# Two tiles in front of the split gated activations get more unused columns

## The chip, the cores and the metric

The kernel runs on one core of one Trainium2 chip. The metric is the device time of one execution in microseconds: 899.65 us as the median of three runs (899.22 to 900.09). One execution was also taken by the hardware profiler; it took 898.85 us, and its trace spans 897.0 us from the first to the last instruction, so 1.85 us lie around the span.

## The reference, cut to what matters

A decoder trunk of two layers works on 256 positions of width 2048 in float32. Each layer has the same wiring:

```
hn = rmsnorm(h, norm_g[l])
z  = hn @ w_in                       # one combined input projection
y  = concat(head outputs) * silu(gate)
h  = h + y @ w_out                   # one output projection
```

Layer 0 has dilated attention heads beside gated linear attention (GLA) heads. Layer 1 has S5 state-space channels beside HGRN2 heads, and its S5 output passes through one more product with a 1024x1024 matrix (`s5_w_glu`). The last step is a final rmsnorm. In this document "gated activation" means `y`, the left operand of the output projection.

## The kernel before, in words

Every large product is made of three TensorE products in the type fp32r. A float32 operand is split into a high part, rounded to fp32r, and a low part, the rest; high times high, high times low and low times high are added up in PSUM. The normalised input is held as `xh` and `xl` (split by `split_x`, L205 and L206), the gated activation as `yh` and `yl`, and a weight tile as `wh` (ScalarE, L168) and `wl` (VectorE, L169), both made from `raw`, which a DMA on SyncE's queue fills 1 MB at a time. All four activation tiles have 16 k-tiles of 256 columns, so one k-tile is 1024 bytes of a partition.

Two helpers run these products. `gemm_fm` (matmuls on L181) makes a block of 512 features by 256 positions: the weight slice of 128x128 is stationary (it is loaded into the array) and the activation k-tile of 256 columns moves. A group in it is 4 k-tiles, and one k-tile is 12 matmuls: three products by four weight slices. `gemm_tm` (L200) makes a block of 256 positions by 512 features: a 128x128 slice of the activation is stationary and 512 weight columns move. The last quarter of the last projection is written out by hand with the same operands in 256 columns (`mms`, L756): in its first half the moving operand is a weight tile `wh` or `wl`, in its second half the moving weights lie in the memory of `xh` and `xl`, which are free by then.

The gated activations are used in these places, and nowhere else on TensorE:

- `out_proj` of layer 0, four blocks of `gemm_fm` with 16 k-tiles: 4 x 16 x 12 = 768 matmuls, with `yh` or `yl` as moving operand.
- the S5 product (`I["wg"]`), two blocks of `gemm_fm` with 8 k-tiles: 192 matmuls, `yh` or `yl` moving.
- the output projection of layer 1, three blocks of `gemm_tm`: 3 x 16 x 6 = 288 matmuls, `yh` or `yl` stationary.
- its last quarter (L756): 192 matmuls, `yh` or `yl` stationary.

The order of instructions on each engine is fixed when the program is built. Small float32 matmuls of the mixers (attention, GLA, S5) and of the norms are put between the large ones in many places, so the stream of large matmuls is cut into stretches.

Tiles lie in SBUF one behind the other in the order of their pools, each rounded up to 32 bytes. This gives the start of each tile in a partition; what matters of the layout of the kernel before is:

| tile | starts at byte | modulo 512 | what lies in front |
|---|---|---|---|
| `hT` (inside `xv`) | 17,392 | 496 | `vec` |
| `xh`, `xl` | 33,792 and 50,176 | 0 | `xv` |
| `wh`, `wl` buffers | from 124,736, each 4096 long | 320 | `raw` |
| `pT` (attention, 392 columns) | 191,520 | 32 | `qk` |
| `yh`, `yl` of layer 0 | 193,088 and 209,472 | 64 | `pT` |
| S5 preparation tiles of layer 0 | from 193,088 | 64 | `pT` |
| gates of layer 0 (in `gq` and `gk`) | 155,456 and 159,552 | 320 | `gf` |
| `gz0`, `gz1` (gates of layer 1; `gz1` has 1048 columns) | 181,280 and 185,376 | 32 | `small` tiles |
| S5 tiles of layer 1 (`tb`, `X`, `t0`...) | from 189,568 | 128 | `gz1` |
| `yh`, `yl` of layer 1 | 189,568 and 205,952 | 128 | `gz1` |

The S5 preparation uses the same memory as `yh` of layer 0 before it, and the S5 tiles the same as `yh` of layer 1. A slice that is a stationary operand (128 columns, 512 bytes) starts at the same place modulo 512 as its tile.

Of the kernel before, what the change touches and what calls it, by code (L numbers as in the profile page):

```python
# [12 lines left out]
F32 = mybir.dt.float32  # L13
# [7 lines left out]
S = 256  # L21
# [36 lines left out]
def trunk(ctx: ExitStack, tc: tile.TileContext, I, out):  # L58
# [13 lines left out]
    def urgent():  # L72
        return tc.high_priority(offset=HI)
# [16 lines left out]
    def pm_tile(name="pm"):  # L90
        return pm.tile([128, 512], F32, name=name, tag="pm")
# [21 lines left out]
    def finish_norm(tag):  # L113
        V.tensor_add(sqa[:, 0:2], sqa[:, 0:2], sqa[:, 2:4])
        V.tensor_add(sqa[:, 0], sqa[:, 0], sqa[:, 1])
        ps = pm_tile()
        for t in range(2):
            T.matmul(ps[:, t:t + 1], sqa[:, 0, t * 128:(t + 1) * 128], ones[:, 0:1], start=True, stop=True)
        ms = small.tile([128, 2], F32, name="nms")
        V.tensor_scalar(ms, ps[:, 0:2], 1.0 / D, EPS, op0=OP.mult, op1=OP.add)  # L120
        rc = const.tile([128, 2], F32, name=tag + "c")
        rsqrt(rc, ms, 2, "nr")
        pb = pm_tile()
        for t in range(2):
            dg = small.tile([128, 128], F32, name="dg")
            V.tensor_scalar(dg, ident, rc[:, t:t + 1], None, op0=OP.mult)
            T.matmul(pb[:, t * 128:(t + 1) * 128], ones, dg, start=True, stop=True)
        rb = const.tile([128, S], F32, name=tag + "b")
        A.activation(rb, pb[:, 0:S], AF.Copy)
        return rc, rb  # L130
# [62 lines left out]
    def gemm_tm(src, groups, ah, al, mid=None, order=None):  # L193
        ps = pg.tile([128, 2, 512], F32, name="pg")
        last = groups * 4 - 1
        for i, kt, wh, wl in _iter(src, groups, mid, order):
            for n, (w, a) in enumerate(((wh, ah), (wh, al), (wl, ah))):
                for t in range(2):
                    ts_ = slice(t * 128, (t + 1) * 128)
                    state["mm"] = T.matmul(ps[:, t], a[:, kt, ts_], w, start=(i == 0 and n == 0),  # L200
                                           stop=(i == last and n == 2), skip_group_check=True)
        return ps
# [8 lines left out]
    def gla_tiles():  # L211
        return (mix.tile([128, 4, S], F32, name="gf"), mix.tile([128, 4, S], F32, name="gq"),
                mix.tile([128, 4, S], F32, name="gk"))

    att = ExitStack()
    ap_ = att.enter_context(tc.tile_pool(name="att", bufs=1))
# [23 lines left out]
    f, q, k = gla_tiles()  # L240
# [167 lines left out]
    def attention(h, q, k, v, vc):  # L408
        pr = ap_.tile([128, 2, S], F32, name="pr", bufs=1)
        mx = small.tile([128, 2], F32, name="amx")  # L410
        den = small.tile([128, 2], F32, name="aden")
        ps = pm_tile().rearrange("p (t j) -> p t j", t=2)
        for t in range(2):
            n = 128 * (t + 1)
            T.matmul(ps[:, t, 0:n], q[:, t * 128:(t + 1) * 128], k[:, 0:n], start=True, stop=True)  # L415
        for t in range(2):
            n = 128 * (t + 1)
            V.scalar_tensor_tensor(pr[:, t, 0:n], ps[:, t, 0:n], rsc[:, t:t + 1], bias[:, t, 0:n],
                                   op0=OP.mult, op1=OP.add)
            V.tensor_reduce(mx[:, t:t + 1], pr[:, t, 0:n], axis=mybir.AxisListType.X, op=OP.max)  # L420
        V.tensor_scalar(mx, mx, -1.0, None, op0=OP.mult)
        for t in range(2):
            n = 128 * (t + 1)
            A.activation(pr[:, t, 0:n], pr[:, t, 0:n], AF.Exp, bias=mx[:, t:t + 1], accum_out=den[:, t:t + 1])
        V.reciprocal(den, den)
        for t in range(2):
            n = 128 * (t + 1)
            V.tensor_scalar(pr[:, t, 0:n], pr[:, t, 0:n], den[:, t:t + 1], None, op0=OP.mult)
        pt = pm_tile()
        for n, (t, j) in enumerate(((0, 0), (1, 0), (1, 1))):  # L430
            T.transpose(pt[:, n * 128:(n + 1) * 128], pr[:, t, j * 128:(j + 1) * 128], ident)
        pT = ap_.tile([128, 384 + 8], F32, name="pT", bufs=1)[:, 0:384]
        A.activation(pT, pt[:, 0:384], AF.Copy)
        po = pm_tile()
        T.matmul(po[:, 0:256], v[:, 0, vc:vc + 128], pT[:, 0:256], start=True, stop=False)
        T.matmul(po[:, 128:256], v[:, 1, vc:vc + 128], pT[:, 256:384], start=False, stop=True)
        A.activation(oT[:, h], po[:, 0:256], AF.Copy)
# [14 lines left out]
    def heads(qk, h):  # L452
        for n in range(2):
            attention(h + n, qk[:, n], qk[:, 2 + n], v, (h + n) * 128)
# [34 lines left out]
    def gate_tm(src, rc, zs):  # L489
        ps = gemm_tm(src, 4, xh, xl)  # L490
        z = zs.rearrange("p a s -> p (a s)").rearrange("p (t d) -> p t d", t=2)
        with urgent():
            for t in range(2):
                A.activation(z[:, t], ps[:, t], AF.Silu, scale=rc[:, t:t + 1])
        return z
# [34 lines left out]
    with urgent():  # L530
        rc1, rb1 = finish_norm("r1")
# [3 lines left out]
    w1 = I["w1"]  # L535
    gz = ctx.enter_context(tc.tile_pool(name="gz", bufs=1))
# [124 lines left out]
    for half in range(2):  # L661
        f, q, k = gla_tiles()
# [4 lines left out]
        for n in range(4):  # L667
# [3 lines left out]
        v = mix.tile([128, 2, 512], F32, name="gv")  # L671
        evac_tm(v, 0, gemm_tm(w1[4 + 3 * half], 4, xh, xl), rc1)
        gla(f, q, k, v, 128, 512 * half)
    zs2 = [gate_tm(w1[10 + n], rc1, gz.tile([128, 4 * S + 24 * n], F32, name=f"gz{n}")[:, 0:4 * S]
                   .rearrange("p (a s) -> p a s", a=4)) for n in range(2)]
    while fillq:
        hook()
# [441 lines left out]
def build(arrays):  # L1119
    nc = bacc.Bacc("TRN2", target_bir_lowering=False, num_devices=1)  # L1120
    I = {k: nc.dram_tensor("in_" + k + "_dram", v.shape, mybir.dt.from_np(v.dtype), kind="ExternalInput").ap()
         for k, v in arrays.items()}
    out = nc.dram_tensor("out_0_dram", (2, 128, D), F32, kind="ExternalOutput").ap()
    with tile.TileContext(nc, schedule_with_timeline_sim=True) as tc:
        trunk(tc, I, out)
    if not nc.is_finalized():
        nc.finalize()
    return nc
# [8 lines left out]
```

## Time and profile before

| | |
|---|---|
| median of three runs | 899.65 us |
| the profiled execution | 898.85 us |
| its span | 897.0 us |
| TensorE (PE) busy | 880.9 us, 98% of the span |
| weight loads (PEld), beside the matmuls | 806.7 us, 90% |
| VectorE (DVE) busy | 636.2 us, 71% |
| ScalarE (ACT) busy | 472.5 us, 53% |
| GpSimd (POOL) busy | 54.4 us, 6% |

A matmul's own duration (about 0.28 us for 256 columns) is longer than the time from its start to the start of the next one, since they are pipelined. What one matmul costs the engine is therefore read from starts: a timeline row gives the start of a group of matmuls, and the difference of two starts over the number of matmuls between them is the interval. PEld is the load of the stationary operand, which runs beside the matmul before it. The granted clock is 1.00 in every stage below but the last.

### The profile page before, as it was taken

Reading aid. Unit: us, or ns where it says so; the run is one execution under the profiler, and the core shown is the slowest. Engines: PE = TensorE matmul, PEld = TensorE weight load, DVE = VectorE, ACT = ScalarE, POOL = GpSimd, SP = SyncE. Lnnn points to the kernel's source line nnn. Section 1 sums busy time; section 2 is a strip of 40 time slices with the busy share of each in tenths; the row PEclk is TensorE's granted clock in tenths of the full one; section 3 lists DMA queues with packets and bytes.
Section 4 is the critical chain, followed back from the end, with each engine's and each line's share of the span. In section 5 each row is a group of like instructions: output and inputs, shape, how many; then the busy total and the mean of one; then the engine's idle time right before and its main releaser. Section 6 shows DMA issues by size and latency. Waiting matters only on the chain.

```text
span 897.0 us, 18689 instructions
## 1 busy us (share of the span) xinstructions
PE 880.9 (98%) x7728; PEld 806.7 (90%) x7728; DVE 636.2 (71%) x1197; ACT 472.5 (53%) x715; POOL 54.4 (6%) x106
## 2 busy tenths in 40 slices
PE   8999999999999999999999999999999999999995
PEld 8987799889998899999999998799877899988894
DVE  7987975889869758756575677776987756665562
ACT  7654546665746756544443335455455475544451
POOL 0001100111101001000000001100110000000000
PEclk9999999999999999999999999999999999999998
DMA  9837744777667546544476665754654554554532
GB/s 317 317 100 213 255 164 143 235 254 236 230 210 257 188 168 230 192 176 177 176 277 225 218 245 188 247 191 165 224 165 152 190 189 175 200 180 172 176 132 94
DMA packets 40388, 180.40 MB, mean 201 GB/s; under 512 B 12720, under 2 KB 14256, under 8 KB 22768
## 3 DMA queue, kind: packets, MB, share of 16 engines
q1 hardware_dynamic: 29440, 154.99, 49.0%
q0 software_dynamic: 7984, 22.69, 7.8%
q10 hardware_dynamic: 2880, 1.54, 0.6%
q8 instruction: 60, 0.98, 0.4%
q14 instruction: 24, 0.20, 0.1%
HBM read 166.48 MB, written 12.71 MB: 200 GB/s over the span
## 4 chain that ended last, share of the span: by engine, by line
PE 88%; DVE 4%; DMA 2%; ACT 2%; issue 2%; SPq 0%; POOL 0%; POOLq 0%; DVEq 0%
PE pg L181 51%; PE pg L200 26%; PE pg L756 2%; PE pm L287 1%; PE pm L339 1%; PE pm L621 1%; DMA E<-ed 1%; PE pm L625 1%; DVE wl L169 1%; DMA raw<-in_w_dram 1%; PE pm L583 1%; PE pm L308 1%; PE pm L415 1%; PE pm L1025 1%; ACT wh L168 1%
## 5 line engine op out<-in xcount | busy, mean ns | idle before, releaser
L168 ACT ACTIVATE wh<-raw 128x1024 fp32r<-128x1024 f32 (+2 forms) x276 | 287.7, 1045 | 324.8 <-PE pg L181 192.4
L169 DVE TENSOR_TENSOR wl<-raw,wh 128x1024 fp32r<-128x1024 f32 (+2 forms) x276 | 332.3, 1206 | 171.5 <-ACT wh L168 166.6
L181 PE MATMUL pg<-xh,wh 128*128 128x256 f32 x1024 | 161.8, 279 | 2.3 <-ACT wh L168 2.3
L181 PE MATMUL pg<-xh,wl 128*128 128x256 f32 x1024 | 163.1, 280 | 0.1
L181 PE MATMUL pg<-xl,wh 128*128 128x256 f32 x1024 | 161.1, 278 | 0.0
L181 PEld LDWEIGHTS pg<-xh,wh 128*128 128x128 f32 x1024 | 136.6, 188 | 4.0 <-ACT wh L168 3.4
L181 PEld LDWEIGHTS pg<-xh,wl 128*128 128x128 f32 x1024 | 136.9, 188 | 1.3 <-DVE wl L169 0.5
L181 PEld LDWEIGHTS pg<-xl,wh 128*128 128x128 f32 x1024 | 136.7, 188 | 0.6 <-issue 0.3
L200 PE MATMUL pg<-wl,xh 128*128 128x512 f32 x320 | 101.0, 396 | 0.7 <-DVE wl L169 0.5
L200 PE MATMUL pg<-wh,xl 128*128 128x512 f32 x320 | 100.7, 394 | 0.0
L200 PE MATMUL pg<-wh,xh 128*128 128x512 f32 x320 | 100.3, 394 | 0.0
L200 PEld LDWEIGHTS pg<-wl,xh 128*128 128x128 f32 x320 | 59.1, 188 | 14.2 <-DVE wl L169 1.6
L200 PEld LDWEIGHTS pg<-wh,xl 128*128 128x128 f32 x320 | 59.8, 188 | 12.9
L200 PEld LDWEIGHTS pg<-wh,xh 128*128 128x128 f32 x320 | 59.3, 188 | 12.8
L181 PE MATMUL pg<-yh,wh 128*128 128x256 f32 x320 | 51.8, 283 | 0.0
L181 PE MATMUL pg<-yh,wl 128*128 128x256 f32 x320 | 51.3, 282 | 0.0
L181 PE MATMUL pg<-yl,wh 128*128 128x256 f32 x320 | 51.3, 282 | 0.0
L181 PEld LDWEIGHTS pg<-yh,wh 128*128 128x128 f32 x320 | 44.1, 191 | 0.0
L181 PEld LDWEIGHTS pg<-yl,wh 128*128 128x128 f32 x320 | 44.0, 191 | 0.0
L181 PEld LDWEIGHTS pg<-yh,wl 128*128 128x128 f32 x320 | 44.0, 191 | 0.0
L965 POOL DMA_DIRECT2D tabs<-pc x44 | 23.8, 546 | 164.9 <-DVE x L975 43.3
L200 PE MATMUL pg<-wh,yh 128*128 128x512 f32 x96 | 30.4, 397 | 0.0
(350 smaller groups left out, 1008.4 us busy)
## 6 DMA issues: line engine op xcount, KB each, us to landing
raw<-in_w_dram SPq DMA_DIRECT2D x100, 1024.0 KB, 4.9
raw<-in_wo_dram SPq DMA_DIRECT2D x28, 1024.0 KB, 4.8
tb<-tabs POOLq DMA_DIRECT2D x8, 768.0 KB, 6.5
tabs<-pc POOLq DMA_DIRECT2D x20, 256.0 KB, 5.4
raw<-in_wg_dram SPq DMA_DIRECT2D x4, 1024.0 KB, 4.8
raw<-in_wo1l_dram SPq DMA_DIRECT2D x4, 1024.0 KB, 4.8
raw<-in_w_dram SPq DMA_DIRECT2D x6, 512.0 KB, 7.5
tabs<-pc POOLq DMA_DIRECT2D x24, 128.0 KB, 4.5
```

Of the source, the lines that this page charges most:

```text
L168: state["wh"] = A.activation(w, r, AF.Copy)
L169: V.tensor_sub(l, r, w)
L181: state["mm"] = T.matmul(ps[:, c], w[:, cs], a[:, kt], start=(i == 0 and n == 0 and c % 2 == 0), stop=(i == last and n == 2), skip_group_c ...
L200: state["mm"] = T.matmul(ps[:, t], a[:, kt, ts_], w, start=(i == 0 and n == 0), stop=(i == last and n == 2), skip_group_check=True)
L287: T.matmul(ps[32 * b:32 * b + 32, t, hd], k[:, hd, r], Q[:, hd, r], start=True, stop=True)
L308: T.matmul(ps[j0:j0 + h, hd, j0 + h:j0 + 2 * h], k[:, hd, b:b + h], Qp[:, hd, b + h:b + 2 * h], start=True, stop=True)
L339: T.matmul(ps[:, (hd - h0) * dv:(hd - h0 + 1) * dv], AT[:, hd, t + j], v[:, j, hd * dv:(hd + 1) * dv], start=(j == 0), stop=(j == t))
L415: T.matmul(ps[:, t, 0:n], q[:, t * 128:(t + 1) * 128], k[:, 0:n], start=True, stop=True)
L583: T.matmul(pv[g * 64:g * 64 + 64, w, pr], t["W"][w][us, 4 * h + pr], X[us, g, 4 * h + pr], start=True, stop=True)
L621: T.matmul(py[g * 64:g * 64 + 64, pr], w[:, pr], X[:, g, pr], start=(pr == 0), stop=False, skip_group_check=True)
L756: T.matmul(ps[:, t, 0:256], a_[:, kt, ts_], w_, start=(kt == 0 and n == 0), stop=(kt == KT - 1 and n == 2), skip_group_check=True)
L965: nc.gpsimd.dma_start(tabs[qt, dst, n], t[src].rearrange("p a b -> p (a b)"))
```

## The change

The attention tile `pT` is allocated with 120 unused columns behind its 384 instead of 8, and `gz1` with 120 unused columns behind its 1024 instead of 24 (`gz0` has none either way).

```diff
-        pT = ap_.tile([128, 384 + 8], F32, name="pT", bufs=1)[:, 0:384]
+        pT = ap_.tile([128, 384 + 120], F32, name="pT", bufs=1)[:, 0:384]
...
-    zs2 = [gate_tm(w1[10 + n], rc1, gz.tile([128, 4 * S + 24 * n], F32, name=f"gz{n}")[:, 0:4 * S]
+    zs2 = [gate_tm(w1[10 + n], rc1, gz.tile([128, 4 * S + 120 * n], F32, name=f"gz{n}")[:, 0:4 * S]
```

In layer 0 what lies behind `pT` moves by 112 columns, 448 bytes: `yh` starts at 193,536 = 378 x 512. In layer 1 what lies behind `gz1` moves by 96 columns, 384 bytes: `yh` starts at 189,952 = 371 x 512. The S5 preparation tiles move with the first, the S5 tiles with the second. No instruction is added, taken away or given another size.

## Rows read from the trace of the kernel before

**Rows 1.** The page: busy time of engines, and the chain that ended last by engine.
```profile
PE 880.9 (98%) x7728; PEld 806.7 (90%) x7728; DVE 636.2 (71%) x1197; ACT 472.5 (53%) x715; POOL 54.4 (6%) x106
PE 88%; DVE 4%; DMA 2%; ACT 2%; issue 2%; SPq 0%; POOL 0%; POOLq 0%; DVEq 0%
```

**Rows 2.** By stage (start:end, us): PE, PEld, DVE, ACT, POOL busy (instructions), clock, DMA.
```profile
361.20:453.30 92.10, 92.10 (x770) 92.10 (x769) 55.20 (x62) 44.64 (x52) 0.00 (x0) 1.00 0.51 184
721.30:747.50 26.20, 26.20 (x227) 26.20 (x226) 14.21 (x24) 17.84 (x42) 0.59 (x1) 1.00 0.55 201
793.60:862.60 69.00, 69.00 (x308) 55.68 (x308) 37.84 (x39) 33.18 (x41) 0.00 (x0) 1.00 0.51 183
```

**Rows 3.** Waits in 361.2 to 453.3 us: total us, times, longest.
```profile
ACT wh L168 <- PE pg L181: 42.6, 25, 1.8
```

**Rows 4.** Timeline of PE, layer 0, entering and near the end of the output projection.
```profile
360.27 0.62 PE L181 MATMUL pg<-xh,wl 128*128 128x256 f32 x4
360.73 0.63 PE L181 MATMUL pg<-yh,wh 128*128 128x256 f32 x4
...
362.15 0.64 PE L181 MATMUL pg<-yh,wh 128*128 128x256 f32 x4
...
451.43 0.64 PE L181 MATMUL pg<-yh,wh 128*128 128x256 f32 x4
```

**Rows 5.** The same for the S5 product of layer 1.
```profile
729.12 0.63 PE L181 MATMUL pg<-yl,wh 128*128 128x256 f32 x4
...
746.08 0.63 PE L181 MATMUL pg<-yl,wh 128*128 128x256 f32 x4
```

**Rows 6.** The gate blocks right behind it: first matmuls, and two later ones.
```profile
747.02 1.91 PE L504 MATMUL pm<-cst,gz 128*128 128x128 f32 x16
748.69 0.71 PE L181 MATMUL pg<-xh,wh 128*128 128x256 f32 x4
...
750.15 0.62 PE L181 MATMUL pg<-xh,wh 128*128 128x256 f32 x4
...
790.95 0.62 PE L181 MATMUL pg<-xh,wh 128*128 128x256 f32 x4
```

**Rows 7.** A stretch with xh behind small matmuls of the norm, layer 1.
```profile
464.02 0.36 PE L118 MATMUL pm<-ones,sqa 128*128 128x1 f32 x2
...
465.62 0.63 PE L181 MATMUL pg<-xh,wh 128*128 128x256 f32 x4
...
471.28 0.63 PE L181 MATMUL pg<-xh,wh 128*128 128x256 f32 x4
```

**Rows 8.** L200, moving 512 columns: stationary xh (layer 0), stationary yh (layer 1).
```profile
167.74 0.62 PE L200 MATMUL pg<-wh,xh 128*128 128x512 f32 x2
...
192.46 0.62 PE L200 MATMUL pg<-wh,xh 128*128 128x512 f32 x2
...
795.52 0.63 PE L200 MATMUL pg<-wl,yh 128*128 128x512 f32 x2
...
815.12 0.64 PE L200 MATMUL pg<-wl,yh 128*128 128x512 f32 x2
```

**Rows 9.** L756: first half (two rows), second half (two rows).
```profile
864.31 0.28 PE L756 MATMUL pg<-wl,yh 128*128 128x256 f32 x1
...
871.38 0.28 PE L756 MATMUL pg<-wl,yh 128*128 128x256 f32 x1
...
881.16 0.28 PE L756 MATMUL pg<-xh,yh 128*128 128x256 f32 x1
...
882.94 0.28 PE L756 MATMUL pg<-xh,yh 128*128 128x256 f32 x1
```

**Rows 10.** Groups by line, all 897 us: busy us, mean ns, idle before.
```profile
L583 PE MATMUL pm<-X,tb 64*64 64x64 f32 x256 | 9.3, 221 | 0.0
L504 PE MATMUL pm<-cst,gz 128*128 128x128 f32 x32 | 4.2, 274 | 0.0
L712 PE MATMUL pm<-cst,xv 128*128 128x128 f32 x32 | 4.1, 272 | 0.0
```

## The prediction

> **What bounds the kernel now.** I read the page first. TensorE is busy 98% of the span, and the chain of work that ended last runs through it for 88% [rows 1]. So the time is a sum over matmuls, and what counts is how often a matmul starts. I then looked at the stages that read `yh` and `yl`, by the table of stages: in layer 0's output projection PE is busy for all of 92.1 us, DVE for 55.2 and ACT for 44.6; in the S5 product and in layer 1's output projection PE is busy throughout as well [rows 2]. What feeds PE runs ahead of it: in the first of these stages ScalarE stood for 42.6 us waiting for PE to give a `wh` buffer back [rows 3], so a faster PE finds its weights ready. Last I read the timeline for the interval between starts, and there the operand's place shows.
>
> - Output projection of layer 0 (`yh` moving, at 64 modulo 512): from 362.15 to 451.43 us lie 62 rounds of 12 matmuls, 89.28 us / 744 = 120.0 ns [rows 4].
> - S5 product (`yh` moving, at 128): 16.96 us / 144 = 117.8 ns [rows 5].
> - Gate blocks right behind it, the same code line and the same `wh` buffers, but `xh` moving, at 0: 40.80 us / 360 = 113.3 ns [rows 6].
> - 512 moving columns: 24.72 us / 108 = 228.9 ns with `xh` stationary (at 0), 19.60 us / 84 = 233.3 ns with `yh` stationary (at 128) [rows 8].
>
> The moment of the change is in the trace: the last four `xh` matmuls in front of the output projection start within 0.46 us (115 ns each), and the projection behind them runs at 120 [rows 4]. Weights, PSUM tiles and code line are the same on both sides; the operand is not, and what differs in it is its place (and its values). One row speaks against a rule as simple as "0 is fast": a stretch with `xh` behind the norm's small matmuls runs at 5.66 us / 48 = 117.9 ns [rows 7]. Going through the starts of all 3072 `xh` matmuls of 256 columns I count some 350 at this slow interval, in nine stretches that each begin behind an interruption; nearly all the rest are at 113.3. So an operand at 0 has two intervals, about nine tenths fast, and an operand at 64 was never seen below 120.
>
> **The change, part by part.** No instruction is added or removed; each part is a count times a difference of intervals.
>
> 1. Output projection of layer 0: 768 matmuls move to 0 modulo 512. At the interval of `xh`: 768 x (120.0 - 113.3) ns = 5.1 us. Nothing cuts into this stage, and it is entered from a fast stretch without a gap [rows 4], so I take the fast interval. The other end is the slow one: 768 x (120.0 - 117.9) = 1.6 us. All of it lies on PE's path. What is late next is the split of weights: DVE would work 55.2 us in 87 instead of in 92.1 [rows 2], which is no bound.
> 2. S5 product: 192 matmuls. At 113.3 it is 192 x 4.45 ns = 0.85 us; at the slow interval nothing. It begins behind small matmuls of GLA, and interruptions have led to either (fast behind L504 [rows 6], slow behind L118 [rows 7]). I take half, 0.4 us.
> 3. Output projection of layer 1: 288 matmuls, now with a stationary operand at 0 as in layer 0: 288 x (233.3 - 228.9) = 1.3 us.
> 4. Its last quarter: 192 matmuls at 7.07 us / 60 = 117.8 ns in the first half and 1.78 us / 15 = 118.7 in the second [rows 9]. Here three matmuls in a row add to the same PSUM columns, which no stage with `xh` does, so the interval may have another reason. Bounds: nothing, and 192 x 4.45 = 0.85 us. I take half, 0.4 us.
> 5. S5 tiles and S5 preparation tiles also move. Their matmuls are plain float32 with 64 columns: 256 on L583 [rows 10], and as many again, by the code, on L621 and L625. The trace has no such matmul at 0, so I bound them by the same 4.45 ns either way, 512 x 4.45 = 2.3 us. The nearest rows are float32 transposes of operands at 320 and 32 (L504) and at 496 (L712): 274 and 272 ns [rows 10]. They show no such step, so I take 0. VectorE, ScalarE and DMA work on these tiles lies beside PE.
>
> Sum: 5.1 + 0.4 + 1.3 + 0.4 = 7.2 us. Against the profiled execution that is a span of 897.0 - 7.2 = 889.8 us and, with the 1.85 us around it, 891.65. This execution lies 0.8 us under the median of the runs, so for the median I take 899.65 - 7.2 = 892.4 us.
>
> [...]
>
> **The rivals.**
>
> *Slow interval.* `yh` at 0 settles at 117.9 ns, as some stretches of `xh` do [rows 7]. Then part 1 is 1.6 us, parts 2 and 4 nothing, part 3 still 1.3: 2.9 us, 896.75 us. For it: the state is chosen at a restart, and I don't know by what. Against it: the projection continues a fast stretch.
>
> *No effect.* The place is not the cause (the values are, or something else that `yh` brings). Then 899.65 us stays. Against it: three places gave three intervals with nothing else in common, and each was constant over its whole stage whatever DVE and ACT did.
>
> *Slower.* The interval follows from how the stream falls into step at a restart, not from the place; `yh` then keeps its 120 ns, and the moved S5 tiles only shift the restarts of layer 1. There lie 8 blocks of 192 `xh` matmuls, 1536. Each one that goes over to the slow interval costs 4.5 ns: from 400 on (1.8 us) the kernel is measurably slower, with half of them it is 768 x 4.5 = 3.5 us, 903.1 us. Against it: gains of 7.2 us would outweigh even all 1536 (6.9 us), so it needs part 1 to fail as well.
>
> **How the numbers follow.** Forecast 0.80, slow interval 0.10, no effect 0.06, slower 0.04. The forecast's own range is 890.4 to 894.5: parts 2 and 4 between their bounds give 891.5 to 893.3, and stretches of `xh` that change their interval (350 x 4.45 ns = 1.6 us are slow now) add about 1.1 to either side. The range asked for takes in the slow interval too: 890.4 to 896.9. A change of 0.2% (1.8 us) is about the least that can be told from none here. The first two cases are both beyond it: faster 0.90, same 0.06, slower 0.04.
>
> **What would show it.** Right: rounds of 12 in layer 0's output projection take 1.36 us instead of 1.44, the stage some 87 us instead of 92.1; layer 1's projection starts a matmul every 228.9 ns. Step 1 is wrong if the interval there is 117.9 or 120; step 3 if 233.3 stays; step 5 if the S5 lines change their means. The whole is wrong if stretches with `xh`, which the change doesn't touch, go over to the slow interval in large numbers, or if PE shows idle time in the projection that it did not have.

## The result, and the profile after

The changed kernel takes 892.62 us (median of four), the kernel before 899.56 us (median of four): 6.9 us less, a ratio of 0.992 with a 95% interval of 0.9901 to 0.994. One of the four runs of the changed kernel took 4931.6 us; the ratio is without it, and the other three have a median of 892.18 us, 7.4 us less. The profiled execution takes 892.18 us with a span of 890.4 us, against 897.0 before.

The order of instructions is the same on every engine, and so are their numbers. The first fence has the page after: busy time of the engines and two of the three groups that have the gated activations as moving operand (line, engine, operation, tiles, shape, count, then busy us and mean ns). Before, the means of these two are 283 and 282 ns.

```profile
PE 874.7 (98%) x7728; PEld 802.0 (90%) x7728; DVE 635.5 (71%) x1197; ACT 472.0 (53%) x715; POOL 54.4 (6%) x106
L181 PE MATMUL pg<-yh,wh 128*128 128x256 f32 x320 | 50.0, 277 | 0.0
L181 PE MATMUL pg<-yl,wh 128*128 128x256 f32 x320 | 49.5, 277 | 0.0
```

PE lost 6.2 us of busy time and its weight loads 4.7; DVE and ACT did the same work (0.7 and 0.5 us less). The next fence is the timeline of PE after (start, length of the group, engine, line, operands, count), in the places that [rows 4] show for before: entering layer 0's output projection, near its end, and the first matmuls behind it.

```profile
359.93 0.62 PE L181 MATMUL pg<-xh,wl 128*128 128x256 f32 x4
360.38 0.62 PE L181 MATMUL pg<-yh,wh 128*128 128x256 f32 x4
...
361.74 0.62 PE L181 MATMUL pg<-yh,wh 128*128 128x256 f32 x4
...
440.62 0.62 PE L181 MATMUL pg<-yh,wh 128*128 128x256 f32 x4
...
447.42 0.62 PE L181 MATMUL pg<-xh,wh 128*128 128x256 f32 x4
```

From 361.74 to 440.62 us lie 58 rounds of 12: 78.88 us / 696 = 113.3 ns, where [rows 4] have 120.0. The whole projection, from its first matmul to the first of the next product, lasts 447.42 - 360.38 = 87.04 us. What feeds it still runs ahead, as the waits between 360.4 and 447.4 us show (total us, times, longest; before in [rows 3]):

```profile
ACT wh L168 <- PE pg L181: 37.0, 23, 1.7
```

The places of [rows 5], [rows 8] and [rows 9] after, in the same columns: the S5 product behind its two interruptions, layer 1's output projection, and the two halves of its last quarter.

```profile
717.63 0.62 PE L181 MATMUL pg<-yl,wh 128*128 128x256 f32 x4
718.99 0.62 PE L181 MATMUL pg<-yl,wh 128*128 128x256 f32 x4
...
722.16 0.64 PE L181 MATMUL pg<-yl,wh 128*128 128x256 f32 x4
739.12 0.63 PE L181 MATMUL pg<-yl,wh 128*128 128x256 f32 x4
...
789.94 0.62 PE L200 MATMUL pg<-wl,yh 128*128 128x512 f32 x2
807.79 0.62 PE L200 MATMUL pg<-wl,yh 128*128 128x512 f32 x2
...
857.55 0.28 PE L756 MATMUL pg<-wl,yh 128*128 128x256 f32 x1
863.91 0.28 PE L756 MATMUL pg<-wl,yh 128*128 128x256 f32 x1
...
874.81 0.28 PE L756 MATMUL pg<-xh,yh 128*128 128x256 f32 x1
876.25 0.28 PE L756 MATMUL pg<-xh,yh 128*128 128x256 f32 x1
```

The S5 product has both intervals: 1.36 us / 12 = 113.3 ns in its first piece, and behind the next GLA matmuls 16.96 us / 144 = 117.8 ns to its end. Layer 1's projection has 17.85 us / 78 = 228.8 ns instead of 233.3. The last quarter is unchanged in its first half (6.36 us / 54 = 117.8) and *slower* in its second: 1.44 us / 12 = 120.0 ns, where [rows 9] have 118.7. With both operands at 0 modulo 512, this is the slowest interval of all. The forecast has no place for that, and the experiments start from it.

### The profile page after: what moved, and what is told of

It is laid out like the page before. It is cut to its first block, busy times and chain, and to the rows that moved or that the text cites. A ratio compares the mean times of both kernels' runs of the same rounds, so it can differ in the third digit from the quotient of the medians.

```text
span 890.4 us, 18689 instructions
## 1 busy us (share of the span) xinstructions
PE 874.7 (98%) x7728; PEld 802.0 (90%) x7728; DVE 635.5 (71%) x1197; ACT 472.0 (53%) x715; POOL 54.4 (6%) x106
## 4 chain that ended last, share of the span: by engine, by line
PE 81%; DVE 6%; DMA 4%; ACT 4%; issue 3%; SPq 0%; POOL 0%; ACTq 0%; POOLq 0%; DVEq 0%
PE pg L181 47%; PE pg L200 24%; DMA raw<-in_w_dram 2%; PE pg L756 2%; DVE wl L169 2%; PE pm L287 1%; PE pm L339 1%; DMA E<-ed 1%; ACT wh L168 1%; PE pm L621 1%; PE pm L625 1%; PE pm L308 1%; PE pm L415 1%; PE pm L1025 1%; ACT bb L1019 0%
## 5 line engine op out<-in xcount | busy, mean ns | idle before, releaser
L200 PE MATMUL pg<-wl,xh 128*128 128x512 f32 x320 | 100.9, 396 | 0.6 <-DVE wl L169 0.6
L200 PE MATMUL pg<-wh,xl 128*128 128x512 f32 x320 | 100.7, 394 | 0.0
L200 PE MATMUL pg<-wh,xh 128*128 128x512 f32 x320 | 100.2, 394 | 0.0
L200 PEld LDWEIGHTS pg<-wl,xh 128*128 128x128 f32 x320 | 59.0, 188 | 14.2 <-DVE wl L169 1.4
L200 PEld LDWEIGHTS pg<-wh,xl 128*128 128x128 f32 x320 | 59.8, 188 | 12.8
L200 PEld LDWEIGHTS pg<-wh,xh 128*128 128x128 f32 x320 | 59.3, 188 | 12.8
L181 PE MATMUL pg<-yh,wh 128*128 128x256 f32 x320 | 50.0, 277 | 0.0
L181 PE MATMUL pg<-yl,wh 128*128 128x256 f32 x320 | 49.5, 277 | 0.0
L181 PE MATMUL pg<-yh,wl 128*128 128x256 f32 x320 | 49.5, 277 | 0.0
L200 PE MATMUL pg<-wh,yh 128*128 128x512 f32 x96 | 30.1, 395 | 0.0
```

Of the source, the lines that this page charges most:

```text
L181: state["mm"] = T.matmul(ps[:, c], w[:, cs], a[:, kt], start=(i == 0 and n == 0 and c % 2 == 0), stop=(i == last and n == 2), skip_group_c ...
```

## Experiments

Two theories. **Place**: an operand is fast where it begins at 0 modulo 512 (the forecast). **Distance**: what counts is how far apart the moving and the stationary operand of a matmul begin. Most experiments move only unused columns. Intervals are read as above: starts many rounds apart, over the matmuls between.

**Layer 0 alone.**

```diff
-    zs2 = [gate_tm(w1[10 + n], rc1, gz.tile([128, 4 * S + 120 * n], F32, name=f"gz{n}")[:, 0:4 * S]
+    zs2 = [gate_tm(w1[10 + n], rc1, gz.tile([128, 4 * S + 24 * n], F32, name=f"gz{n}")[:, 0:4 * S]
```

> Only the columns behind pT are added, so only yh of layer 0 moves to 0 modulo 512; layer 1 keeps its places. If the place of the operand sets the interval, layer 0's output projection runs at 113.3 ns (stage 87 us instead of 92.1) and layer 1's output projection stays at 233.3 ns: 899.6 - 5.1 = 894.4 us. If the gain comes from somewhere else (the S5 tiles that move with gz1, the phases of restarts), the time stays within 1.5 us of 892.6 or goes back to 899.6.

Measured: 894.41 us, a ratio of 0.9949 (0.9927 to 0.997) to the kernel before, which took 899.37 us beside it: 5.0 us less. Timeline of PE in layer 0's projection:

```profile
370.31 0.62 PE L181 MATMUL pg<-yh,wh 128*128 128x256 f32 x4
430.15 0.62 PE L181 MATMUL pg<-yh,wh 128*128 128x256 f32 x4
```

It runs at 59.84 us / 528 = 113.3 ns, with layer 1's tiles where they lay before. So the time came from this product; the S5 tiles and layer 1 take no part in these 5 us. That the median met the 894.4 us expected is luck: the ten runs lie between 892.49 and 899.82 us, two of them at 899.8, and no trace shows why.

**Other places for yh.** Two kernels put other numbers of unused columns behind `pT` and `gz1` (the second has 88 and 56).

```diff
-        pT = ap_.tile([128, 384 + 120], F32, name="pT", bufs=1)[:, 0:384]
+        pT = ap_.tile([128, 384 + 56], F32, name="pT", bufs=1)[:, 0:384]
...
-    zs2 = [gate_tm(w1[10 + n], rc1, gz.tile([128, 4 * S + 120 * n], F32, name=f"gz{n}")[:, 0:4 * S]
+    zs2 = [gate_tm(w1[10 + n], rc1, gz.tile([128, 4 * S + 8 * n], F32, name=f"gz{n}")[:, 0:4 * S]
```

> yh of layer 0 lies at 256 modulo 512, yh of layer 1 at 64, weights at 320 as ever. Place theory (what counts is whether the activation begins at 0 modulo 512): layer 0's projection at 117.8 or 120.0 ns, not 113.3; layer 1's with its stationary operand at 64 at 233.3 ns or more; total 898 to 901 us. Distance theory (what counts is how far apart, modulo 512, the moving operand and the weights begin; 0 against 320 is fast, 64 against 320 and 128 against 320 are slow): 256 against 320 is a distance not seen yet in a large product, so 113.3 is possible there. A rule by 256 bytes (half of 512 does as well) would give 113.3 ns in layer 0.

> yh of layer 0 lies at 384 modulo 512, yh of layer 1 at 256, weights at 320. Place theory: layer 0's projection at 117.8 or 120.0 ns, layer 1's at 233.3 ns or more, 898 to 901 us. Distance theory: 384 is 64 behind the weights, open. A rule by 128 bytes would give 113.3 in layer 0 and 228.9 in layer 1; a rule by 256 bytes 228.9 in layer 1 alone.

Timeline of PE in the first of them (yh at 256 in layer 0, at 64 in layer 1): layer 0's projection, layer 1's, and the second half of the last quarter.

```profile
370.91 0.62 PE L181 MATMUL pg<-yh,wh 128*128 128x256 f32 x4
430.75 0.62 PE L181 MATMUL pg<-yh,wh 128*128 128x256 f32 x4
...
793.41 0.61 PE L200 MATMUL pg<-wl,yh 128*128 128x512 f32 x2
809.73 0.61 PE L200 MATMUL pg<-wl,yh 128*128 128x512 f32 x2
...
877.94 0.28 PE L756 MATMUL pg<-xh,yh 128*128 128x256 f32 x1
881.00 0.28 PE L756 MATMUL pg<-xh,yh 128*128 128x256 f32 x1
```

yh at 256 runs at 59.84 us / 528 = 113.3 ns, exactly as at 0. And 64, the slowest place as a moving operand, is the best as a stationary one: 16.32 us / 72 = 226.7 ns with 512 moving columns, and 3.06 us / 27 = 113.3 ns in the last quarter. In the second kernel yh at 384 runs at 117.8 ns like 128, and at 256 its layer 1 has the 228.9 ns of 0. A single execution took 894.68 us with the first kernel and 899.92 with the second. The second was no faster than the kernel before, although its products with `yh` took 3.6 us less from start to start. Its `xh` matmuls took 5.9 us more (367.7 against 361.8): some 3 us of it are waits, 2.1 of them behind the late transfer of the last section, and 1.7 us the gate blocks of layer 1, at the same addresses and behind the same L504 as in [rows 6]:

```profile
750.68 0.64 PE L181 MATMUL pg<-xh,wh 128*128 128x256 f32 x4
793.08 0.64 PE L181 MATMUL pg<-xh,wh 128*128 128x256 f32 x4
```

42.40 us / 360 = 117.8 ns, where [rows 6] have 113.3. The place theory by 512 has fallen; what is left repeats by 256 and points to the pair of operands.

**The weights moved instead.** Columns behind the last constant tile move `raw`, `wh` and `wl`; `pT` and `gz1` get 72 unused columns each, so that yh stays at 0 in both layers.

```diff
-    part = const.tile([128, 2], F32, name="part")
+    part = const.tile([128, 56], F32, name="part")[:, 0:2]
```

> Unused columns behind the last constant tile put raw, wh and wl at 0 modulo 512 instead of 320; yh and xh stay at 0 in both layers (the other two columns are cut to make up for the 192 bytes). Place theory: every large operand now begins at 0; the 256-column products stay at 113.3 ns, those with 512 moving columns can only gain (228.9 ns down to about 226, the fastest start that the trace shows, 1248 of them: up to 3 us): 889 to 893 us. Distance theory: moving operand and weights begin at the same place, as in the second half of the last quarter of the changed kernel, which runs at 120.0 ns: all 4032 products of 256 columns at 120 ns cost 6.7 ns each, 27 us, about 920 us.

Measured: 912.47 us, a ratio of 1.015 (1.0135 to 1.0165). Timeline of PE: a block with `xh` of layer 0 and the output projection behind it.

```profile
350.44 0.64 PE L181 MATMUL pg<-xh,wh 128*128 128x256 f32 x4
356.20 0.64 PE L181 MATMUL pg<-xh,wh 128*128 128x256 f32 x4
...
370.61 0.64 PE L181 MATMUL pg<-yh,wh 128*128 128x256 f32 x4
431.08 0.64 PE L181 MATMUL pg<-yh,wh 128*128 128x256 f32 x4
```

Both run at 120.0 ns (5.76 us / 48 and 60.47 us / 504), with every activation at 0 modulo 512 as the place theory wants it. With 512 moving columns it is 226.7 ns. The total lies some 7 us under the 920 expected: I had counted all 4032 matmuls of 256 columns from 113.3 ns, though several hundred were slower already, and took nothing off for the 1248 products of 512 columns that gain 2.2 ns each (up to 2.8 us).

**The distances between.** Three places of `yh` (unused columns behind `pT` and `gz1`: 0 and 0, 48 and 48, 104 and 40).

> No unused columns behind pT and gz1: yh of both layers at 32 modulo 512, weights at 320. The place theory has fallen (yh at 256 runs at 113.3 ns, and yh at 0 at 120 when the weights lie at 0 too). What is left is the distance theory: the start of the moving operand less that of the stationary one, modulo 256. 256 moving columns so far: 192 gives 113.3 or 117.8, 0 gives 120.0, 64 gives 117.8, 128 some 118.5 in the last quarter alone; 512 moving columns: 0 gives 226.7, 64 228.9, 192 233.3. Here layer 0's projection has a distance of 32 - 320 = 224, between the fastest (192) and the slowest (0): 113.3 if there is a step, about 116.7 if it is a slope. Layer 1's projection has 320 - 32 = 32: between 226.7 and 228.9 ns.

> yh of both layers at 224 modulo 512. Distance modulo 256 in layer 0's projection 224 - 320 = 160, between 128 (118.5 ns) and 192 (113.3): 113.3 to 118.5; in layer 1's 320 - 224 = 96, between 64 (228.9) and 192 (233.3). A theory by the absolute start has no number for it, other than that it isn't 0 or 256 and so is slow, 117.8 or 120 ns.

> yh of layer 0 at 448, of layer 1 at 192 modulo 512: the distance is 128 for both projections. Distance theory: layer 0 as the second half of the last quarter before, about 118.5 ns, and if a constant one, 117.8; layer 1 between 228.9 and 233.3 ns. If the 118.5 ns of the last quarter came from its three sums in a row into the same PSUM columns, layer 0 runs at another interval here.

Layer 0's projection in the three kernels, in this order (distances 224, 160 and 128):

```profile
370.77 0.64 PE L181 MATMUL pg<-yh,wh 128*128 128x256 f32 x4
430.41 0.64 PE L181 MATMUL pg<-yh,wh 128*128 128x256 f32 x4
...
370.49 0.63 PE L181 MATMUL pg<-yh,wh 128*128 128x256 f32 x4
430.30 0.64 PE L181 MATMUL pg<-yh,wh 128*128 128x256 f32 x4
...
370.22 0.64 PE L181 MATMUL pg<-yh,wh 128*128 128x256 f32 x4
430.03 0.64 PE L181 MATMUL pg<-yh,wh 128*128 128x256 f32 x4
```

59.64 us, 59.81 us and 59.81 us over 504 matmuls: 118.3, 118.7 and 118.7 ns. All three are slow, so it is neither a step nor a slope: of the eight distances in steps of 32 only 192 reached 113.3. Layer 1's projection at distance 32 ran at 233.3 ns, not between 226.7 and 228.9 as expected. Single executions took 901.29, 899.58 and 899.42 us.

**The same slow places, made fast by the weights alone.** `yh` goes back to 64 in layer 0 and 128 in layer 1, as before the change, and the weights move by 64 bytes.

```diff
-    part = const.tile([128, 2], F32, name="part")
+    part = const.tile([128, 18], F32, name="part")[:, 0:2]
...
-    zs2 = [gate_tm(w1[10 + n], rc1, gz.tile([128, 4 * S + 120 * n], F32, name=f"gz{n}")[:, 0:4 * S]
+    zs2 = [gate_tm(w1[10 + n], rc1, gz.tile([128, 4 * S + 8 * n], F32, name=f"gz{n}")[:, 0:4 * S]
```

> Weights at 384 modulo 512 (64 more than before), yh of layer 0 at 64 and of layer 1 at 128, exactly the places that they have before the change; xh at 0. Distance theory (start of the moving operand less that of the stationary one, modulo 256): layer 0's projection 64 - 384 = 192, so 113.3 ns at the place that ran at 120.0; layer 1's 384 - 128 = 0, so 226.7 ns at the place that ran at 233.3; the S5 product 128 - 384 = 0, so 120.0; all products of xh with 256 columns 0 - 384 = 128, so some 118.6 instead of 113.3 (3072 x 5.3 = up to 16 us lost), with 512 columns 384 - 0 = 128, about 232.7. Total about 911 us. Place theory: 120.0, 233.3, 117.8 for yh and 113.3 for xh as before the change, 899 us.

Timeline of PE: `xh` in layer 0, layer 0's projection, layer 1's.

```profile
350.48 0.64 PE L181 MATMUL pg<-xh,wh 128*128 128x256 f32 x4
356.17 0.64 PE L181 MATMUL pg<-xh,wh 128*128 128x256 f32 x4
...
370.39 0.62 PE L181 MATMUL pg<-yh,wh 128*128 128x256 f32 x4
430.23 0.62 PE L181 MATMUL pg<-yh,wh 128*128 128x256 f32 x4
...
808.06 0.62 PE L200 MATMUL pg<-wl,yh 128*128 128x512 f32 x2
824.38 0.62 PE L200 MATMUL pg<-wl,yh 128*128 128x512 f32 x2
```

`yh` at 64 runs at 59.84 us / 528 = 113.3 ns instead of 120.0, and at 128 as stationary operand at 16.32 us / 72 = 226.7 instead of 233.3, while `xh`, still at 0, falls to 5.69 us / 48 = 118.5. A single execution took 909.83 us, 911 expected. Each of these intervals came as the distance theory had it. One series of `xh` in layer 1 did not, though its distance is the same 128:

```profile
478.43 0.65 PE L181 MATMUL pg<-xh,wh 128*128 128x256 f32 x4
511.55 0.65 PE L181 MATMUL pg<-xh,wh 128*128 128x256 f32 x4
```

33.12 us / 276 = 120.0 ns, so 192 is not the only distance with two intervals.

Behind the first matmuls of a stretch, the large products of these kernels have the intervals of one table, by the start of the moving operand less that of the stationary one, modulo 256 bytes:

| distance | 256 moving columns, ns | 512 moving columns, ns |
|---|---|---|
| 0 | 120.0 | 226.7 |
| 32 | 116.7 | 233.3 |
| 64 | 117.8 | 228.9 |
| 96 | 120.0 | 233.3 |
| 128 | 118.5 to 118.8, or 120.0 behind some restarts | 232.4 to 232.6, or 233.3 behind some restarts |
| 160 | 118.7 in layer 0's projection, 117.3 in the S5 product | not run |
| 192 | 113.3, or 117.8 behind some restarts | 233.3 |
| 224 | 118.3 | not run |

(32 and 96 with 256 columns are from the last quarter of the kernels with `yh` at 32 and 224.) Before the change `yh` lay 64 - 320 = 0 and 128 - 320 = 64 from the weights and `xh` 0 - 320 = 192; the change put `yh` at 192 too. All weight slices begin at the same place modulo 256, and the next slice is loaded beside each matmul (before the change PEld and PE are both busy for all of the 92.10 us of layer 0's projection, and the loads for four `yl` matmuls begin at 399.95 us, those matmuls at 400.07), so these runs don't tell whether a matmul's own weights or the next ones count. Why the distance matters stays open.

**A place of its own for 512 columns.** Of the distances that were run, 192 has the shortest interval for 256 moving columns (113.3 ns) and 0 for 512 (226.7), and one weight buffer serves both. So each buffer gets 64 more columns, and the start in it depends on the product.

```diff
-            wh = stream.tile([128, 2, 512], F32R, name="wh", bufs=3)
-            wl = stream.tile([128, 2, 512], F32R, name="wl", bufs=3)
+            wh, wl = [stream.tile([128, 1024 + 64], F32R, name=n, bufs=3)[:, off:off + 1024]
+                      .rearrange("p (k c) -> p k c", k=2) for n in ("wh", "wl")]
...
-            gw = sp_.tile([128, 2, S], F32, name="gw")
+            gw = sp_.tile([128, 2, S], F32, name="gw", tag="ys")
```

(`off` is 0 in `gemm_fm` and 48 in `gemm_tm`; the last quarter's first half begins at column 32; `pT` and `gz1` have 56 unused columns.)

> The changed kernel, but each wh and wl buffer has 64 more columns, and where 512 weight columns move (gemm_tm) the tile begins 192 bytes further in, so that distance 0 holds there (226.7 ns) while gemm_fm keeps distance 192 (113.3 ns); in the last quarter's first half it begins 128 bytes further in (distance 192, 113.3 instead of 117.8). To make room gw shares the memory of ys. Distance theory: (960 + 288) x 2.2 ns = 2.8 us and 96 x 4.45 ns = 0.4 us less than the changed kernel: about 889.4 us. Place theory by 512: nothing or a loss, since the weights' place changes only for some products: 892.6 us or more.

> The changed kernel as it is, on the same chip and between the same runs of the kernel before: 892 to 893 us, as a measure for the run before it in this list. Its stretches of xh that fall into the slow interval may differ from one execution to the next by a microsecond or two, though nothing in the program does; layer 0's projection stays at 113.3 ns.

Measured beside one another: 892.00 us, a ratio of 0.9924 (0.9905 to 0.9943), and for the changed kernel itself 892.94 us, 0.9933 (0.9912 to 0.9954). The first is 2.6 us more than the 889.4 expected, and the intervals overlap, so whether this version is better stays unclear. The interval of 512 columns did come down, but not at once behind a restart (timeline of PE in this version):

```profile
164.68 0.63 PE L200 MATMUL pg<-wh,xh 128*128 128x512 f32 x2
166.07 0.62 PE L200 MATMUL pg<-wh,xh 128*128 128x512 f32 x2
...
185.11 0.62 PE L200 MATMUL pg<-wh,xh 128*128 128x512 f32 x2
190.55 0.62 PE L200 MATMUL pg<-wh,xh 128*128 128x512 f32 x2
```

1.39 us / 6 = 231.7 ns at the start of the stretch, 5.44 us / 24 = 226.7 later. Many stretches of `gemm_tm` are shorter than that, which eats a part of the 2.8 us; and the first half of the last quarter, now at distance 192, took the slow interval of 117.8 ns, so its 0.4 us did not come. Added up from start to start, the products of 512 columns take 290.1 us in this profile and 292.0 in that of the changed kernel, 1.9 us of the 2.8; but `xh` with 256 columns took 0.7 us more and L287 0.9, and the spans are 890.3 and 890.4 us.

## Why the prediction was right, and where its reason was not

The forecast was 892.4 us, a gain of 7.2; measured were 892.62 and 6.9. The first and third steps carry the gain and came as forecast; that the sum came so close is in part luck, as the others show. By its steps:

1. *Layer 0's projection, 5.1 us.* Right: 92.14 us (360.73 to 452.87 before) became 87.04, 5.1 us, and layer 0 alone gave 5.0 us in the total. That it was decided by entering the stage at the fast interval, as argued, is not shown: with the weights moved by 64 bytes the stage is entered from `xh` at 118.5 ns and runs at 113.3 all the same.
2. *S5 product, 0.4 us.* Too much. Only its first 24 matmuls are fast, the other pieces still start every 117.8 ns: 24 x 4.45 ns = 0.1 us.
3. *Layer 1's projection, 1.3 us.* Right: 288 x (233.3 - 228.8) = 1.3 us.
4. *Last quarter, 0.4 us.* Wrong in sign. The first half kept its interval; the second, with both operands at 0, went from 118.7 to 120.0 ns, 96 x 1.3 = 0.1 us lost. The reason that I offered, three sums in a row into the same PSUM columns, also fell: at distance 192 the same three sums run at 113.3.
5. *S5 tiles, 0.* Right: L583, L621 and L625 have means of 221, 246 and 242 ns before and after, and from start to start each line's sum is the same within 0.02 us.

These steps add up to 5.1 + 0.1 + 1.3 - 0.1 = 6.4 us; the span fell by 6.6. The rest is what stretches of `xh` and small matmuls did in these two executions (below).

The step that failed is the reading of the cause. "At 0 modulo 512" was right for this kernel only because its weights lie at 320: in these runs the interval went with the distance between the two operands modulo 256 bytes, and layer 0's projection took 120.0 ns at 0 and 113.3 at 192, whether `yh` or the weights were moved. The trace of before had a hint that I did not weigh: in the last quarter `xh` at 0 was the moving operand and still ran at 118.7 ns [rows 9], and I gave that to PSUM. Of the rivals, "slow interval" happened in most of the S5 product alone; "no effect" and "slower" did not happen. What "slower" rested on, a stretch that takes one of two intervals behind a restart, was seen (113.3 and 117.9 ns behind L415, below), but was small here: added up from start to start, waits between them included, the 3072 `xh` matmuls of 256 columns take 361.8 us in the profiled execution before and 362.8 after, a loss of 1.0 us and not of 3.5. All of it fell in stretches before 361 us; those of layer 1, which the rival named, took the same time in both (within 0.02 us each). It can be larger: the gate blocks of the kernel with `yh` at 384 and 256 lost 1.7 us at one restart. Small matmuls happened to take 1.4 us less (L287 14.5 and 13.5 us, the first matmuls on L238 3.7 and 3.3), which is how the span still fell by 6.6.

## What to carry to other kernels

Read the interval between matmul starts, not the busy share: an engine at 98% still held 0.8% here. Where two products of the same shape run at different steady intervals, compare where their operands begin, both of them and relative to one another, before giving a rule for one. An experiment that moves the partner (the weights) instead of the suspect is what tells a place from a distance.

## What the runs showed of the hardware that was not expected

**One distance, two intervals.** At distance 192, 256 columns start, behind the first matmuls of a stretch, every 113.3 or every 117.8 ns until the next interruption. The stretch of `xh` behind the attention matmuls (L415) at about 250 us is the same work at the same addresses in both kernels, and its interval differs. Timeline of PE before:

```profile
250.18 0.62 PE L181 MATMUL pg<-xh,wl 128*128 128x256 f32 x4
251.54 0.62 PE L181 MATMUL pg<-xh,wl 128*128 128x256 f32 x4
```

and after:

```profile
249.48 0.63 PE L181 MATMUL pg<-xh,wl 128*128 128x256 f32 x4
252.31 0.63 PE L181 MATMUL pg<-xh,wl 128*128 128x256 f32 x4
```

1.36 us / 12 = 113.3 ns against 2.83 us / 24 = 117.9. What decides at a restart stays open; a stretch of 60 matmuls is worth 0.3 us, the 384 of the gate blocks 1.7, and over all stretches, waits included, the two executions differ by 1.0 us (361.8 and 362.8).

**A late DMA cost twice in one execution.** The profiled execution of the changed kernel's second run took 896.26 us, with layer 0's projection as fast as ever. The first line of its waits on PE (total us, times, longest) and of those on DVE between 580 and 600 us, and the table of two stretches there (busy us of PE, PEld, DVE, ACT, POOL with their counts, granted clock, DMA share and GB/s):

```profile
PE pm L287 <- DVE gk L325: 3.1, 2, 2.3
...
DVE gw L643 <- ACT gw L642: 4.3, 1, 4.3
...
585.00:590.00 5.00, 4.88 (x43) 4.68 (x41) 1.48 (x3) 0.56 (x1) 0.00 (x0) 1.00 0.91 356
590.00:595.00 5.00, 2.79 (x73) 2.75 (x74) 4.23 (x7) 3.65 (x6) 0.00 (x0) 0.75 0.08 28
```

VectorE stood for 4.3 us at the GELU of an S5 quarter (`gw`, L643), whose input had come back late from DRAM (5.6 us from issue to landing, where the first profile of the changed kernel has 4.2 and that of the kernel before 3.9); GLA's next step (`gk`, L325) waits behind it in VectorE's order, and PE behind that, for 2.3 us. Then the granted clock was 0.75 from 590 to 595 us, where PE was busy for 2.79 us of five, having been 1.00 from 585 to 590; the 35 `xh` matmuls from 593.09 us took 5.5 us, in the first profile of the changed kernel 4.2. The unused columns are not the cause: the kernel with `yh` at 32, which has none behind `pT` and `gz1`, shows the same wait of PE (1.9 us) and the lower clock behind it (0.66 from 595 to 600 us). Layer 0 alone (1.9 us), `yh` at 256 and 64 (1.8) and `yh` at 384 and 256 (2.1) show the wait with the clock left at 1.00. What makes the transfer late in one execution and not in another stays open; it is the next thing to look at.
